# A hybrid encoder: the band's mask written into the bias rows, and the product of output and gate queued behind the product of weights and 1/z

## The chip, the cores and the metric

The kernel runs as one program on one core of one Trainium2 chip. The metric is the device time of one execution in microseconds (us), median of three runs. TensorE (PE, with its weight loads, PEld), VectorE (DVE), ScalarE (ACT), GpSimd (POOL) and SyncE (SP) each work through a queue of their own in order; semaphores tie them together. Almost all DMAs are issued by SP.

## The reference

The reference computes a two-layer encoder over x (1024 tokens x 1024 features), with 256 memory tokens. Layer 0 projects the normalised input to three groups of heads and a gate. Group A is banded attention: token i sees token j only where |i-j| <= 128, each head has a learned sink logit, and a relative-position bias (a table of 32 buckets x 6 heads) is added. Group B is dense attention with rotary positions, group X attention into the memory. What the change touches is this:

```python
rel = c - BLOCK - a                       # key minus query, c in 0..383, a in 0..127
bias = rel_bias_lookup(table, rel)
valid = ((jnp.abs(rel) <= WINDOW)[None] & (kpos >= 0)[:, None, :] & (kpos < S)[:, None, :])
logits = jnp.where(valid[None, :, None, None], logits + bias, NEG_INF)
...
p = jax.nn.softmax(jnp.concatenate([logits, sink_col], axis=-1), axis=-1)[..., :-1]
y = jnp.concatenate([y_a, y_b, y_x], axis=-1) * jax.nn.silu(gate)
return x + y @ w_out
```

Layer 1 has a differential attention (group C), with the same bias over all keys, and again X. A last RMS norm ends it.

## The kernel before, in words

Every projection is a chain of 24 fp32r matmuls of 512 columns into `acc` (high part of the activations with high part of the weights, and two cross terms, line 329). The weights come by DMA as `wr`, and are split into `wh` (DVE, line 241) and `wl` (mostly POOL, line 243). The projections are cut into pieces that the loop `run_steps` lays between the steps of attention, so that PE has work while a step's softmax runs on DVE, ACT and POOL. Once they are done, pieces of layer 0's output projection (`pre`, line 702) take their place.

A step of group B (`b_step`) handles one head and one block of 128 queries: scores into `sb` on PE, the minimum `mn` on DVE, the exponential `e` with its sum `z` on ACT, `rz` = 1/z on DVE and then the product `e` = `e` x `rz` (128x1024) on POOL, line 1114. SP copies `e` to `er`, PE transposes it (`te`), ACT and DVE split the result into `PTh` and `PTl`, and every second step PE multiplies with V (`ob`). A step of group A (`a_step`) does this for two query blocks over at most 384 keys each: scores `sa`, on DVE in one instruction the bias `ab` and the minimum (line 1184), on ACT the exponential, on POOL two products with `rz` (line 1198). There are three buffers of `e`; one is free again when the DMA to `er` that reads it has landed.

`y_evac` empties the output accumulator: ACT copies one half, DVE adds the other into `yt`, and POOL multiplies `yt` with the gate `gy` in place (line 473). After the second head of a pair `store_y` writes the gate tile out as `ysc`; the output projection reads it back as `yr` and splits it into `yh` (ACT) and `yl` (DVE).

The bias: a one-hot matrix turns the negated table into one vector of 512 values per head (`vp`, `vs`, `vec_d`). `skew(h)` writes that vector 128 times into `skew_d[h]` in DRAM, and a read with a row pitch of 511 gives each query its shifted row. For group A `a_bias(h)` reads 384 columns into `ab` and adds a 128x384 mask (0 in the band, 1e30 outside) on POOL, line 1152, six times in all. Layer 1 reads the same rows, without a mask, into `toep`.

Inside a step the order is: `s1` (scores, minimum, exponential), pieces of projections, `s3` of an earlier step (which ends with `y_evac`), `s2` of another (transposes and splits), then `finish` (1/z and the product with it), and pieces again. The order on each engine comes from a scheduler that starts from this order; `tc.issue_after(x)` tells it to put an instruction behind x. Each DMA bears one of eight semaphore lanes in turn and SP issues a DMA only when the one eight before it is done.

Of the kernel before, what the change touches and what calls it, by code (L numbers as in the profile page):

```python
# [41 lines left out]
PRE = ((((2, 3, 4, 5), 4), ((6,), 6), ((7,), 6)), (((2, 3), 6), ((4,), 6)))  # L42
SPARE = 24
LATE = 22
# [111 lines left out]
def encoder_kernel(ctx, tc, A):  # L156
# [35 lines left out]
    nsink = const.tile([P, 6], F32, name="nsink")  # L192
    tab = const.tile([32, 6], F32, name="tab")
    edge = pool(ctx, "edge", "right").tile([P, 120], F32, name="edge")
    spare = const.tile([P, SPARE], F32, name="spare")
    for t in (spare, edge):
# [14 lines left out]
            for l in range(2)]  # L211
    vec_d = dr.tile([6, 512], F32, name="vec_d")
    skew_d = dr.tile([6, P, 512], F32, name="skew_d")

# [252 lines left out]
    def y_evac(M, acc, gt, hr, c0, n=256):  # L467
        a = slice(hr * 64, hr * 64 + 64)
        b = slice(64 - hr * 64, 128 - hr * 64)
        t = M.at.tile([P, 256], F32, tag="yt", name="yt", bufs=2)  # L470
        nc.scalar.copy(t[a, :n], acc[b, :n])
        nc.vector.tensor_tensor(out=t[a, :n], in0=acc[a, :n], in1=t[a, :n], op=ALU.add)
        nc.gpsimd.tensor_tensor(out=gt[a, c0:c0 + n], in0=t[a, :n], in1=gt[a, c0:c0 + n], op=ALU.mult)

    def run_steps(steps, jobs, hooks=None, pace=None):
# [4 lines left out]
        for i in range(n + LAG + 1):  # L480
# [37 lines left out]
            if finish:  # L518
                with (tc.issue_after(behind.ins) if behind is not None else nullcontext()):
                    finish()  # L520
                finish = None
            if jobs is not None:
                jobs.pull(f // 2)
                if hooks:
                    hooks(-1)
# [510 lines left out]

    dma(tab, A["rel_bias"])
    nc.vector.tensor_scalar(out=tab, in0=tab, scalar1=-1.0, scalar2=None, op0=ALU.mult)
    oh = sg(M, "oh", F32)[:32, :]
    dma(oh, A["onehot"])  # L1040
    vp = ps_t("vp")
    nc.tensor.matmul(vp[0:6, :], tab, oh, start=True, stop=True)
    vs = sg(M, "vs", F32)[:6, :]
    nc.vector.tensor_copy(vs, vp[0:6, :])
    dma(vec_d, vs)
# [34 lines left out]
    if True:  # L1080
        def b_step(h, qb):
# [8 lines left out]
            def s1(h=h, qb=qb, e=e):  # L1090
# [20 lines left out]
                def finish():  # L1111
                    rz = stat("rz")
                    nc.vector.reciprocal(rz, z)  # L1113
                    nc.gpsimd.tensor_tensor(out=et, in0=et, in1=rz.to_broadcast([P, 1024]), op=ALU.mult)  # L1114
                    e[0] = et
# [4 lines left out]
            if st.sub == 1:  # L1120
                def s3(h=h, qb=qb, grp=grp):
                    ph, pl_ = grp["pt"]
                    acc = ps_a("ob")[:, :256]
                    n = 0
                    for kt in range(8):
                        for pt in (ph, pl_):
                            nc.tensor.matmul(acc, B["v"][:, kt, h // 3, :], pt[:, kt, :],
                                             start=(n == 0), stop=(n == 15))
                            n += 1
                    y_evac(M, acc, gates[3 + h // 2], h % 2, (qb - 1) * P)  # L1130
                    if h % 2 == 1 and qb == 7:
                        store_y(0, KORD[0].index(3 + h // 2), gates[3 + h // 2])
                st.s3 = s3
                st.need3 = ("bv", "g%d" % (3 + h // 2))
# [5 lines left out]
    def open_ab():  # L1140
        top_stack.close()
        ab = pool(top_stack, "ab", "right")
        mask = ab.tile([P, 384], F32, name="mask")
        dma(mask, A["mask"])
        abias["mask"], abias["pool"] = mask, ab
        M.xpool, M.xbufs = ab, XB

    def a_bias(h):
        mask = abias["mask"]
        t = abias["pool"].tile([P, 384], F32, tag="ab", name="ab", bufs=2)  # L1150
        dma(t, skew_src(h))
        nc.gpsimd.tensor_tensor(out=t, in0=t, in1=mask, op=ALU.add)
        abias[h] = t

    if True:
        def a_step(h, p):
# [5 lines left out]
            def s1(h=h, p=p, e=e):  # L1162
# [27 lines left out]
                def finish():  # L1190
                    rz = stat("rz2", 2)
                    nc.vector.reciprocal(rz, z)
                    for j in range(2):
# [3 lines left out]
                        ej = et[:, j, c:c + hi - lo]  # L1197
                        nc.gpsimd.tensor_tensor(out=ej, in0=ej, in1=rz[:, j:j + 1].to_broadcast([P, hi - lo]), op=ALU.mult)
                    e[0] = et
# [25 lines left out]
            def s3(h=h, p=p, grp=grp):  # L1225
# [15 lines left out]
                if h % 2 == 1 and p == 3:  # L1241
                    store_y(0, KORD[0].index(h // 2), gates[h // 2])
            st.s3 = s3
# [9 lines left out]
    def hooks0(i):  # L1253
        if 2 <= i < 8:
            skew(i - 2)
        if i < 0:
            wout_hook(0, jobs, "g2", r1)
# [7 lines left out]
    def out_proj(l, hT_next, stack, ahead=None):  # L1265
# [50 lines left out]
        for i, t in enumerate(order):  # L1316
# [31 lines left out]
            if tail:  # L1348
                nc.scalar.activation(xs[:, 0:384], xs[:, 0:384], AF.Identity, scale=r)
                nc.vector.tensor_scalar(out=xs[:, 384:1024], in0=xs[:, 384:1024], scalar1=r, scalar2=None,  # L1350
                                        op0=ALU.mult)
                nc.scalar.dma_start(out=out_d[rows, 0:384], in_=xs[:, 0:384])
                dma(out_d[rows, 384:1024], xs[:, 384:1024])
            elif l == 0:
# [281 lines left out]
def _constants():  # L1636
# [16 lines left out]
    b = np.where(rel > 0, 16, 0) + np.where(n < 8, n, large)  # L1653
    onehot = (np.arange(32)[:, None] == b[None, :]).astype(np.float32)
    r = np.arange(384)[None, :] - 128 - np.arange(128)[:, None]
    mask = np.where(np.abs(r) <= 128, 0.0, 1e30).astype(np.float32)
    return dict(cosT=cosT, sinT=sinT, onehot=onehot, mask=mask)

# [15 lines left out]
```

## Time and profile before

| | |
|---|---|
| three runs | 1227.74 us median (1226.81 to 1227.98) |
| the profiled execution | 1230.69 us |
| its span, first to last instruction | 1228.9 us |
| outside the span in it | 1.8 us |
| PE / DVE / ACT / POOL busy | 1196.5 / 801.1 / 663.1 / 436.3 us |

The span is cut in engines' busy time and waits. A view of waits names who waited for whom; a timeline lists instructions by start, with the idle time in front of each and what ended it in square brackets; a table of windows gives each engine's busy time in a stretch, and the mean clock granted to PE (1.00 is 2.4 GHz; its lower level is 1.2 GHz).

### The profile page before, as it was taken

The numbers are of one execution on the slowest core, as the hardware profiler recorded it, in microseconds if no ns is written. First come the engines' busy times: TensorE is split into PE (matmuls) and PEld (weight loads), VectorE is DVE, ScalarE is ACT, GpSimd is POOL, SyncE is SP. The second block draws the span as 40 slices with busy tenths as digits, with TensorE's granted clock in tenths as the row PEclk, the third lists the DMA queues.
The fourth block names the chain that finished last, engine by engine and source line by source line (L and its number), as shares of the span: only waits on it lengthen the run. The fifth ranks groups of instructions, "written<-read, shape, count | busy, mean of one in ns | idle before, by whom it ended". The sixth has DMA issues, their size and how long they took to land.

```text
span 1228.9 us, 19560 instructions
## 1 busy us (share of the span) xinstructions
PE 1196.5 (97%) x6614; PEld 988.4 (80%) x6614; DVE 801.1 (65%) x1495; ACT 663.1 (54%) x1477; POOL 436.3 (36%) x414
## 2 busy tenths in 40 slices
PE   6999999999999999999999999999999999999997
PEld 5788888888888777888888777777787777777886
DVE  5547665377778878635365866766767767667544
ACT  6248754366667766636157744555545454445332
POOL 5023365366665455437112222333143231301100
PEclk9999999999999999999999999999999999999999
DMA  6664445545465565457645445355363452468354
GB/s 257 200 194 147 163 172 163 166 160 207 163 233 209 208 227 191 151 196 237 186 158 156 153 146 164 121 183 163 124 187 125 153 171 105 149 212 285 121 192 155
DMA packets 114304, 216.70 MB, mean 176 GB/s; under 512 B 13302, under 2 KB 47478, under 8 KB 114204
## 3 DMA queue, kind: packets, MB, share of 16 engines
q1 hardware_dynamic: 114060, 215.25, 52.5%
q8 instruction: 53, 0.87, 0.3%
q14 instruction: 47, 0.39, 0.1%
q10 hardware_dynamic: 144, 0.20, 0.0%
HBM read 87.71 MB, written 39.86 MB: 104 GB/s over the span
## 4 chain that ended last, share of the span: by engine, by line
PE 47%; DVE 2%; DMA 1%; issue 1%; ACT 1%; POOL 0%; POOLq 0%; SPq 0%; DVEq 0%; ACTq 0%
PE acc L329 24%; PE po L702 5%; PE oc L1545 3%; PE sc L1505 3%; PE te L580 3%; PE sc L1514 2%; PE pre L702 2%; PE oc L1547 2%; DMA wr<-in_w_in 1%; PE ssqc L1563 1%; PE ox L656 0%; PE rbcc L1576 0%; PE tv L439 0%; PE sx L543 0%; DVE e L1520 0%
## 5 line engine op out<-in xcount | busy, mean ns | idle before, releaser
L329 PE MATMUL acc<-h,wh 128*128 128x512 f32 x1536 | 499.5, 398 | 1.6 <-DVE h L351 0.8
L329 PEld LDWEIGHTS acc<-h,wh 128*128 128x128 f32 x1536 | 282.4, 188 | 65.7 <-issue 7.9
L329 PE MATMUL acc<-h,wl 128*128 128x512 f32 x768 | 303.8, 396 | 1.5 <-POOL wl L243 1.2
L243 POOL TENSOR_TENSOR wl<-wr,wh 128x512 fp32r<-128x512 f32 x94 | 124.8, 1329 | 286.3 <-DVE wh L241 155.0
L1523 ACT ACTIVATE e<-e,mn 128x1024 f32<-128x1024 f32 x96 | 110.0, 1148 | 117.0 <-DVE mn L1520 116.9
L329 PEld LDWEIGHTS acc<-h,wl 128*128 128x128 f32 x768 | 144.3, 188 | 34.9 <-issue 4.4
L1114 POOL TENSOR_TENSOR e<-e,rz 128x1024 f32<-128x1024 f32 x48 | 91.6, 1910 | 84.2 <-DVE rz L1113 57.8
L1520 DVE CUSTOM_DVE_ANT_0 e<-sc,toep 128x1024 f32<-128x1024 f32 x96 | 113.5, 1218 | 8.0 <-PE sc L1514 7.3
L580 PEld LDWEIGHTS te<-identr,er 128*128 128x128 f32 x896 | 92.2, 143 | 18.8 <-PE sa L543 2.2
L580 PE MATMUL te<-identr,er 128*128 128x128 f32 x896 | 99.9, 246 | 4.3 <-DVE O L1578 1.4
L348 DVE TENSOR_TENSOR PT<-te,PT 128x512 fp32r<-128x512 f32 x112 | 74.3, 687 | 42.8 <-ACT PT L347 39.2
L241 DVE CAST wh<-wr 128x512 fp32r<-128x512 f32 x112 | 58.2, 522 | 42.9 <-PE acc L329 17.3
L348 DVE TENSOR_TENSOR PTl<-te,PTh 128x512 fp32r<-128x512 f32 x112 | 74.0, 684 | 9.4 <-ACT PTh L347 8.9
L1545 PE MATMUL oc<-PT,v 128*128 128x512 f32 x192 | 69.8, 403 | 0.7 <-DVE ckl L1420 0.7
L1532 DVE SCALAR_TENSOR_TENSOR e<-e,mr 128x1024 f32<-128x1024 f32 x48 | 66.3, 1381 | 1.5
L347 ACT CAST PT<-te 128x512 fp32r<-128x512 f32 x112 | 62.7, 589 | 7.2 <-PE te L580 6.7
L347 ACT CAST PTh<-te 128x512 fp32r<-128x512 f32 x112 | 62.2, 586 | 7.9 <-PE te L580 7.1
L702 PE MATMUL po<-woh,yh 128*128 128x512 f32 (+1 forms) x172 | 65.7, 382 | 0.0
L702 PE MATMUL po<-woh,yl 128*128 128x512 f32 (+1 forms) x172 | 65.5, 381 | 0.0
L702 PE MATMUL po<-wol,yh 128*128 128x512 f32 (+1 forms) x172 | 65.3, 380 | 0.0
L1105 DVE TENSOR_REDUCE mn<-sb 128x1 f32<-128x1024 f32 x48 | 58.3, 1216 | 7.0 <-PE sb L543 6.6
L350 ACT ACTIVATE yh<-yr 128x256 fp32r<-128x256 f32 (+2 forms) x56 | 24.0, 447 | 66.2 <-DMA yr<-ysc 37.5
(211 smaller groups left out, 2358.7 us busy)
## 6 DMA issues: line engine op xcount, KB each, us to landing
er<-e SPq DMA_DIRECT2D x112, 512.0 KB, 3.0
wr<-in_w_in SPq DMA_DIRECT2D x96, 256.0 KB, 3.0
ysc<-gy SPq DMA_DIRECT2D x16, 512.0 KB, 2.7
cq<-sg SPq DMA_DIRECT2D x64, 128.0 KB, 2.5
ck<-sg SPq DMA_DIRECT2D x48, 128.0 KB, 2.3
er<-e SPq DMA_DIRECT2D x12, 384.5 KB, 2.6
xpsc<-xh SPq DMA_DIRECT2D x18, 256.0 KB, 2.6
xr<-xpsc SPq DMA_DIRECT2D x9, 512.0 KB, 3.6
```

The costliest lines, as they stand in the source:

```text
L243: (nc.vector if fast else nc.gpsimd).tensor_tensor(out=lo, in0=raw, in1=hi, op=ALU.subtract)
L329: lastmm[0] = nc.tensor.matmul(acc, a, b[:, k, c0:c0 + n], start=(i == 0), stop=(i == 23))
L347: nc.scalar.copy(hi, src)
L348: return nc.vector.tensor_tensor(out=lo, in0=src, in1=hi, op=ALU.subtract)
L580: nc.tensor.transpose(to[:, i * P:(i + 1) * P], e[0][:, k * P:(k + 1) * P], idt)
L702: lastmm[0] = nc.tensor.matmul(acc, a, b, start=(start and n == 0), stop=(stop and n == 2))
L1105: nc.vector.tensor_reduce(out=mn, in_=Sp, op=ALU.min, axis=AX.X)
L1114: nc.gpsimd.tensor_tensor(out=et, in0=et, in1=rz.to_broadcast([P, 1024]), op=ALU.mult)
L1520: nc.vector.tensor_tensor_reduce(out=et, in0=Sp, in1=toeps[h][:, w0:w0 + 1024], scale=1.0, scalar=BIG, op0=ALU.add, op1=ALU.min, accum_out ...
L1523: nc.scalar.activation(et, et, AF.Exp, bias=mn[:, m:m + 1], scale=-1.0, accum_out=z[:, m:m + 1])
L1532: nc.vector.scalar_tensor_tensor(out=es[0], in0=es[1], scalar=c, in1=es[0], op0=ALU.mult, op1=ALU.add)
L1545: nc.tensor.matmul(acc, V[:, kt, 0, :], ph.both[:, kt, :], start=(kt == 0), stop=(kt == 7), skip_group_check=True)
```

## The change

There are four edits. The mask moves into the bias vector: the table becomes 33 rows x 12 columns (the six heads twice; row 33 is 0 for the first six and, once negated, 1 for the last six), the one-hot matrix gets a row 33 with 0 in the band and 1e30 outside, and so the matmul makes six plain and six masked vectors. `skew` writes twelve tiles; A reads the masked ones, and the add and the mask tile are gone. The product of output and gate, and the store behind it, are held in a list `late` and are issued after the step's `finish`, behind the last product with `rz`. `spare` gets smaller by what `tab` grows, so that all other tiles keep their addresses. And the last store of the result goes out on SP in both its parts, 640 columns first; before, ACT issued the part of 384 columns.

```diff
-SPARE = 24
+SPARE = 16
-    tab = const.tile([32, 6], F32, name="tab")
+    tab = const.tile([33, 12], F32, name="tab")
-    vec_d = dr.tile([6, 512], F32, name="vec_d")
-    skew_d = dr.tile([6, P, 512], F32, name="skew_d")
+    vec_d = dr.tile([12, 512], F32, name="vec_d")
+    skew_d = dr.tile([12, P, 512], F32, name="skew_d")
...
-        nc.gpsimd.tensor_tensor(out=gt[a, c0:c0 + n], in0=t[a, :n], in1=gt[a, c0:c0 + n], op=ALU.mult)
+        def mult():
+            with (tc.issue_after(lastw[0].ins) if lastw[0] is not None else nullcontext()):
+                nc.gpsimd.tensor_tensor(out=gt[a, c0:c0 + n], in0=t[a, :n], in1=gt[a, c0:c0 + n], op=ALU.mult)
+        late.append(mult)
+    late, lastw = [], [None]
...
+            while late:
+                late.pop(0)()
...
-    dma(tab, A["rel_bias"])
+    for i in range(2):
+        dma(tab[:32, 6 * i:6 * i + 6], A["rel_bias"])
+    dma(tab[32:33, :], A["onehot"][32:33, 512:524])
-    nc.tensor.matmul(vp[0:6, :], tab, oh, start=True, stop=True)
+    nc.tensor.matmul(vp[0:12, :], tab, oh, start=True, stop=True)
...
-                    nc.gpsimd.tensor_tensor(out=et, in0=et, in1=rz.to_broadcast([P, 1024]), op=ALU.mult)
+                    lastw[0] = nc.gpsimd.tensor_tensor(out=et, in0=et, in1=rz.to_broadcast([P, 1024]), op=ALU.mult)
-                        store_y(0, KORD[0].index(3 + h // 2), gates[3 + h // 2])
+                        late.append(lambda: store_y(0, KORD[0].index(3 + h // 2), gates[3 + h // 2]))
...
-        mask = ab.tile([P, 384], F32, name="mask")
-        dma(mask, A["mask"])
-        dma(t, skew_src(h))
-        nc.gpsimd.tensor_tensor(out=t, in0=t, in1=mask, op=ALU.add)
+        dma(t, skew_src(6 + h))
...
-            skew(i - 2)
+            skew(6 + i - 2)
+        if 10 <= i < 16:
+            skew(i - 10)
...
-                nc.scalar.dma_start(out=out_d[rows, 0:384], in_=xs[:, 0:384])
-                dma(out_d[rows, 384:1024], xs[:, 384:1024])
+                for h in (slice(384, 1024), slice(0, 384)):
+                    dma(out_d[rows, h], xs[:, h])
```

The order on PE and on DVE stays as it was, but for the sizes of the bias vectors' instructions. On POOL the six adds go, and only from the last of them on does the order of the rest change. There, near the end of layer 0's attention, the rows before were these (`e<-e,rz` is the product with 1/z, `gy<-yt,gy` that with the gate):

```order
L1198 TENSOR_TENSOR e<-e,rz_5053 128x256
L473 TENSOR_TENSOR gy<-yt,gy 64x256
L1152 TENSOR_TENSOR ab<-ab,mask 128x384
L473 TENSOR_TENSOR gy<-yt,gy 64x256
L1114 TENSOR_TENSOR e<-e,rz 128x1024 x2
L1198 TENSOR_TENSOR e<-e,rz_5237 128x256
L1198 TENSOR_TENSOR e<-e,rz_5237 128x384
```

and now they are:

```order
L1205 TENSOR_TENSOR e<-e,rz_5053 128x256
L476 TENSOR_TENSOR gy<-yt,gy 64x256
L1125 TENSOR_TENSOR e<-e,rz 128x1024
L476 TENSOR_TENSOR gy<-yt,gy 64x256
L1125 TENSOR_TENSOR e<-e,rz 128x1024
L1205 TENSOR_TENSOR e<-e,rz_5237 128x256
L1205 TENSOR_TENSOR e<-e,rz_5237 128x384
```

The add is gone, and the second product with the gate stands behind the first of the two products with 1/z. From there on each product with the gate stands behind the product with 1/z that it stood in front of, where it did.

On SP, in the first steps of attention (group X, which has no products with 1/z on POOL), the writes of `skew_d` and the loads of weights stood so:

```order
L175 DMA skew_d<-vec_d 128x512 x5
L175 DMA wr<-in_w_in 128x512 x2
L175 DMA er<-e 128x1024
L175 DMA wr<-in_w_in 128x512 x2
L175 DMA er<-e 128x1024
```

and now stand so:

```order
L175 DMA skew_d<-vec_d 128x512 x5
L175 DMA wr<-in_w_in 128x512 x2
L175 DMA skew_d<-vec_d 128x512 x2
L175 DMA er<-e 128x1024
L175 DMA skew_d<-vec_d 128x512
L175 DMA wr<-in_w_in 128x512
L175 DMA skew_d<-vec_d 128x512 x2
L175 DMA wr<-in_w_in 128x512
L175 DMA skew_d<-vec_d 128x512
L175 DMA er<-e 128x1024
```

Five of the six new writes stand in front of the second half of the next weight tile.

Also on SP, near the end of layer 0's attention, the store of a pair of heads and the loads of it stood so:

```order
L175 DMA ysc_94<-gy 128x1024
L175 DMA xpsc_97<-xh 128x512
L175 DMA er<-e 128x769
L175 DMA er<-e 128x1024
L175 DMA xh<-in_x 128x512
L175 DMA yr<-ysc_94 128x2x128
L175 DMA er<-e 128x1024
L175 DMA xpsc_97<-xh 128x512
L175 DMA yr<-ysc_94 128x4x128
```

and now:

```order
L175 DMA xpsc_97<-xh 128x512
L175 DMA ysc_94<-gy 128x1024
L175 DMA er<-e 128x769
L175 DMA er<-e 128x1024 x2
L175 DMA xh<-in_x 128x512
L175 DMA xpsc_97<-xh 128x512
L175 DMA yr<-ysc_94 128x2x128
L175 DMA yr<-ysc_94 128x4x128
```

The first load of `yr` now waits behind a store of `xpsc` (a finished piece of the output projection) that it stood in front of.

## Rows read from the trace of the kernel before

**Rows 1.** The page's busy time by engine, share of the span.
```profile
PE 1196.5 (97%) x6614; PEld 988.4 (80%) x6614; DVE 801.1 (65%) x1495; ACT 663.1 (54%) x1477; POOL 436.3 (36%) x414
```

**Rows 2.** PE's waits, 100 to 600 us: us in total, times, longest.
```profile
PE sa L543 <- DVE mn L1184: 3.7, 3, 2.2
```

**Rows 3.** Windows: busy PE, PEld, DVE, ACT, POOL (instructions), PE clock, DMA share, GB/s.
```profile
75.00:80.00 5.00, 5.00 (x27) 4.29 (x26) 1.99 (x3) 3.15 (x10) 0.00 (x0) 1.00 0.98 329
...
300.00:350.00 50.00, 50.00 (x312) 43.51 (x311) 38.29 (x76) 34.53 (x83) 31.04 (x28) 1.00 0.49 176
...
435.00:440.00 5.00, 3.16 (x23) 2.65 (x21) 1.19 (x5) 2.12 (x6) 4.76 (x4) 1.00 0.50 201
440.00:445.00 5.00, 4.61 (x22) 4.18 (x23) 3.71 (x10) 2.47 (x7) 0.83 (x2) 0.66 0.68 240
```

**Rows 4.** Timeline of PE around two waits: start, us, instruction, [idle before, releaser].
```profile
437.77 0.39 PE L543 MATMUL sb<-bkl,q 128*128 128x512 f32 x1
440.39 0.69 PE L543 MATMUL sa<-ak,q 128*128 128x384 f32 x1 [2.23 <-DVE mn L1184]
...
464.77 0.39 PE L543 MATMUL sa<-ak,q 128*128 128x256 f32 x1 [1.07 <-DVE mn L1184]
```

**Rows 5.** Timeline of DVE, the same stretch.
```profile
432.15 0.15 DVE L1113 RECIPROCAL rz<-z 128x1 f32<-128x1 f32 x1
432.23 0.67 DVE L290 TENSOR_TENSOR wol<-wor,woh 128x512 fp32r<-128x512 f32 x1
...
439.70 0.62 DVE L1184 CUSTOM_DVE_ANT_0 e<-sa,ab,nsink 128x384 f32<-128x384 f32 x1 [3.04 <-DMA er<-e]
```

**Rows 6.** Timeline of SP, the same stretch.
```profile
436.59 2.32 SPq L175 DMA_DIRECT2D er<-e  x2
```

**Rows 7.** Timeline of POOL, the same stretch.
```profile
432.21 1.56 POOL L1152 TENSOR_TENSOR ab<-ab,mask 128x384 f32<-128x384 f32 x1 [3.79 <-DMA ab<-skew_d]
433.85 0.73 POOL L473 TENSOR_TENSOR gy<-yt,gy 64x256 f32<-64x256 f32 x1
434.67 3.75 POOL L1114 TENSOR_TENSOR e<-e,rz 128x1024 f32<-128x1024 f32 x2
```

**Rows 8.** The six adds of the mask: ns min/median/max, first and last start.
```profile
L1152 POOL TENSOR_TENSOR ab<-ab,mask x6: 1008/1017/1564, 218.7 to 432.2; 128x384 f32<-128x384 f32 x6
```

**Rows 9.** Timeline of POOL, two products beside a split on DVE.
```profile
405.99 1.89 POOL L1114 TENSOR_TENSOR e<-e,rz 128x1024 f32<-128x1024 f32 x1 [2.95 <-issue]
...
421.27 2.21 POOL L1114 TENSOR_TENSOR e<-e,rz 128x1024 f32<-128x1024 f32 x1 [3.64 <-issue]
```

**Rows 10.** Timeline of DVE, the split beside the first of these.
```profile
406.08 2.35 DVE L290 TENSOR_TENSOR wol<-wor,woh 128x512 fp32r<-128x512 f32 x1 [0.22 <-ACT woh L289]
```

**Rows 11.** Timeline of SP where the new writes go in.
```profile
70.55 3.06 SPq L175 DMA_DIRECT2D skew_d<-vec_d  x5
...
81.80 2.04 SPq L175 DMA_DIRECT2D wr<-in_w_in  x2
```

**Rows 12.** The writes of skew_d: us from issue to landing.
```profile
DMA to landing us min/median/max: 4.2/4.5/6.2
```

**Rows 13.** Timeline of DVE, the cast of the second half of those weights.
```profile
86.54 0.43 DVE L241 CAST wh<-wr 128x512 fp32r<-128x512 f32 x1 [1.68 <-DMA wr<-in_w_in]
```

**Rows 14.** Timeline of PE, the next wait behind that cast.
```profile
95.12 1.05 PE L833 MATMUL ssq<-small,sq 128*128 128x2 f32 x8 [0.22 <-DVE PTl L348]
```

**Rows 15.** Timeline of SP, the first load of yr and the store of xpsc behind it.
```profile
451.46 0.72 SPq L175 DMA_DIRECT2D yr<-ysc  x1
...
454.33 0.32 SPq L175 DMA_DIRECT2D xpsc<-xh  x1
```

**Rows 16.** Timeline of ACT, the split that reads it.
```profile
461.14 0.42 ACT L350 ACTIVATE yh<-yr 128x256 fp32r<-128x256 f32 x1
```

**Rows 17.** Timeline of the last stores of the result.
```profile
1217.07 8.15 SPq L175 DMA_DIRECT2D out<-xs  x2
...
1224.95 0.38 ACTq L1352 DMA_DIRECT2D out<-xs  x1
```

More of the change, by code (lines that the diff above doesn't have):

```diff
@@ L1033, in encoder_kernel @@
             dma(memT_d[i][:, 4 * j:4 * j + 4, :], memT[i].tiles[j])
-    dma(tab, A["rel_bias"])
+    for i in range(2):
+        dma(tab[:32, 6 * i:6 * i + 6], A["rel_bias"])
+    dma(tab[32:33, :], A["onehot"][32:33, 512:524])
     nc.vector.tensor_scalar(out=tab, in0=tab, scalar1=-1.0, scalar2=None, op0=ALU.mult)
-    oh = sg(M, "oh", F32)[:32, :]
-    dma(oh, A["onehot"])
+    oh = sg(M, "oh", F32)[:33, :]
+    dma(oh, A["onehot"][:, 0:512])
     vp = ps_t("vp")
-    nc.tensor.matmul(vp[0:6, :], tab, oh, start=True, stop=True)
-    vs = sg(M, "vs", F32)[:6, :]
-    nc.vector.tensor_copy(vs, vp[0:6, :])
+    nc.tensor.matmul(vp[0:12, :], tab, oh, start=True, stop=True)
+    vs = sg(M, "vs", F32)[:12, :]
+    nc.vector.tensor_copy(vs, vp[0:12, :])
     dma(vec_d, vs)
@@ L1142, in open_ab @@
         ab = pool(top_stack, "ab", "right")
-        mask = ab.tile([P, 384], F32, name="mask")
-        dma(mask, A["mask"])
-        abias["mask"], abias["pool"] = mask, ab
+        abias["pool"] = ab
         M.xpool, M.xbufs = ab, XB
     def a_bias(h):
-        mask = abias["mask"]
         t = abias["pool"].tile([P, 384], F32, tag="ab", name="ab", bufs=2)
-        dma(t, skew_src(h))
-        nc.gpsimd.tensor_tensor(out=t, in0=t, in1=mask, op=ALU.add)
+        dma(t, skew_src(6 + h))
         abias[h] = t
@@ L1197, in finish @@
                         ej = et[:, j, c:c + hi - lo]
-                        nc.gpsimd.tensor_tensor(out=ej, in0=ej, in1=rz[:, j:j + 1].to_broadcast([P, hi - lo]), op=ALU.mult)
+                        lastw[0] = nc.gpsimd.tensor_tensor(out=ej, in0=ej, in1=rz[:, j:j + 1].to_broadcast([P, hi - lo]), op=ALU.mult)
                     e[0] = et
@@ L1241, in s3 @@
                 if h % 2 == 1 and p == 3:
-                    store_y(0, KORD[0].index(h // 2), gates[h // 2])
+                    late.append(lambda: store_y(0, KORD[0].index(h // 2), gates[h // 2]))
             st.s3 = s3
@@ L1653, in _constants @@
     b = np.where(rel > 0, 16, 0) + np.where(n < 8, n, large)
[L1654 to L1657, printed above, removed]
+    onehot = np.zeros((33, 524), np.float32)
+    onehot[:32, :512] = np.arange(32)[:, None] == b[None, :]
+    onehot[32, :512] = np.where(n <= 128, 0.0, 1e30)
+    onehot[32, 518:] = -1
+    return dict(cosT=cosT, sinT=sinT, onehot=onehot)
 def kernel(**inputs):
```

## The prediction

> **What bounds the kernel now.** I read the page's busy time first: PE is busy for 97% of the span, no other engine for more than 65% [rows 1]. Time can be won only where PE waits or runs at its lower clock, so the view of PE's waits comes next. Between 100 and 600 us, where everything in this change but its first and last DMAs lies, one line leads: the scores of group A (`sa`) waited three times for DVE's line 1184, 3.7 us in all, the longest 2.2 us [rows 2]. The windows then show where PE has no slack to give: from 300 to 350 us it is busy for 50.00 of 50 us [rows 3], although the six adds of the mask are spread over 218.7 to 432.2 us, about 1.0 us each [rows 8]. In most of its six places the add is thus paid by nobody.
>
> The last of the six is another matter. In 435 to 440 us PE is busy for only 3.16 us, and in the next window its clock is 0.66 on average [rows 3]. The timelines give the chain, and the reader should follow it backwards. PE's `sa` starts at 440.39 after 2.23 us of idleness; its work before it ended at 437.77 + 0.39 = 438.16 [rows 4]. It waited for DVE's line 1184, which started at 439.70 and itself stood 3.04 us waiting for a DMA `er<-e`, because only then was a buffer of `e` free to write into [rows 5]. SP issued that copy at 436.59 [rows 6], which is 3.11 us before 439.70. The copy had to wait for POOL's product of `e` with 1/z: the first of the two that start at 434.67 takes half of 3.75 us and ends at 436.55 [rows 7]. And this product was late not for its operand, since `rz` started at 432.15 and took 0.15 us [rows 5]; POOL was standing in the add of the mask, which began at 432.21 after 3.79 us of waiting for its own DMA and took 1.56 us, and then in the product with the gate, 0.73 us [rows 7].
>
> **The change, part by part.**
>
> *The add and the gate's product at 432 us.* Both leave the front of that first product. It then starts when `rz` is there: 432.30, and 0.13 us for the signal. Its duration is 1.89 to 2.21 us [rows 9]; I take 2.21, since DVE has just begun a split of two operands at 432.23 [rows 5], the situation of the 2.21. So it ends at 434.64 instead of 436.55, and the copy is issued 1.9 us sooner. With the same 3.11 us to DVE, `sa` starts at 438.5, against PE's own readiness at 438.16: the wait shrinks from 2.23 to about 0.35 us, a gain of 1.9. What is late next is the same chain; its floor for PE is the 438.16.
>
> *The clock behind it.* A mean of 0.66 over 440 to 445 [rows 3] between levels of 1.0 and 0.5 means 3.4 us at the half, so 1.7 us of work lost. At the wait of 1.07 us at 464.77 [rows 4] I see no such drop, so a wait of 0.35 us should keep the full clock. The bounds are 0 (the clock falls all the same) and 1.7; the nearer row is the shorter wait, so 1.7. The two gains together: 3.6 us.
>
> *The other five adds.* Their POOL time goes, some 5 us, but PE waits for none of it [rows 3]. I take 0. DVE's line 1184 now waits for the DMA of `ab` itself, which landed well before each use, as the add did.
>
> *The order of the gate's products elsewhere.* Up to 425 us POOL's order is the same without the adds. Later, each product with the gate passes behind one with 1/z; those that gave way are 0.73 us long [rows 7], and PE waited for none of the others there except at 464.77, where the wait comes from DVE. 0, with 0.7 us of gain as the other end.
>
> *Six more writes of `skew_d`.* Five of them stand before the second half of the weight pair that SP issues from 81.80 to 83.84 [rows 11]. SP's issue of five such writes took 3.06 us [rows 11] and fits into its idle time. But the 16 DMA engines were full from 75 to 80 us, 0.98 busy at 329 GB/s [rows 3], at which rate a write of 256 KB takes 0.8 us. DVE already stands 1.68 us for that half at 86.54 [rows 13], and the score minimum behind that cast feeds exponentials, casts and splits without a gap, up to PE's `ssq` at 95.12, which waits 0.22 us for them [rows 14]. So what the weights lose, PE loses. The lower end is 0: the DMA engines drain between 80 and 84 us. The upper end: all five writes at up to 1.7 us each (five of them landed within 6.2 us of the last issue [rows 12], 8.6 us after the first), which is rival 3. Two writes are issued directly before the half, 1.6 us of transfer at the full rate, and start some 1.2 us earlier; I take 0.5 us of loss.
>
> *The table and vectors.* Two more small loads and twelve rows in place of six; the matmul still has 512 columns. 0: the loads were issued 10 us before they are used.
>
> *The last store.* SP's second store of the last rows was issued in a group that ends at 1217.07 + 8.15 = 1225.22 [rows 17]; ACT issued its part at 1224.95 beside it. Now the smaller part comes behind, 1225.22 instead of 1224.95, with nothing left to hide it: a loss of 0.3 us, between 0 (the larger part lands last anyway) and 0.6 us (its 192 KB alone at 329 GB/s).
> The Trainium skill (DMA: Bandwidth & Descriptors, Issuing engines are not separate DMA queues) says that DMAs from either engine run on the same 16 DMA engines, and that a second issuer saves only issue time. By that rule the price is the 0.3 us of issue; if ACT's queue had moved its data on its own, it would be the 0.6. No row here separates the two.
>
> **Sum.** -1.9 - 1.7 + 0.5 + 0.3 = -2.8 us. On the profiled execution's own time, span 1228.9 and 1.8 around it, that is 1230.7 - 2.8 = 1227.9. That execution was 3.0 us longer than the median of the runs, 1227.74, with which the change will be compared: 1227.74 - 2.8 = 1224.9 us.
>
> **Rivals.**
>
> *1. More is won.* The other waits of `sa` on line 1184 (3.7 - 2.23 = 1.5 us [rows 2]) shrink as well, because POOL is less often in the way. For it: the same line, the same kind of buffer. Against it: at 464.77 I find DVE, not POOL, late. 1224.9 - 1.5 = 1223.4 us.
>
> *2. POOL's product, now earlier, stalls DVE.* The product of 405.99 us kept a split on DVE that began 0.09 us later busy for 2.35 us instead of 0.67 [rows 5, 9, 10]. If the freed product gets in front of the split of 432.23, DVE is 1.7 us later with line 1184 for the step before, and PE waits some 1.5 us for that at about 434.5. For it: the two now start within 0.2 us of each other. Against it: `rz` signals after the split has started, and then POOL is the one that stretches. 1224.9 + 1.5 = 1226.4 us.
> The Trainium skill (GPSIMD Engine Reference, 1. Specifications) says POOL's SBUF interfaces are shared with VectorE and contend with DVE instructions that have two SBUF inputs. By that rule one of the two must stretch; the trace agrees, with 2.35 us beside 0.67.
>
> *3. Slower: the writes of `skew_d` hold up the weights.* If a write costs the DMA engines 1.7 us and not 0.8, five cost 8.5 us; the backlog from 80 us then reaches past 88, and the second half of the weights lands 3.6 us later. PE waits 3.8 us at 95.12 and the clock falls, 1.7 us more as above. In place of my 0.5 us stand 5.3 to 5.9 us: 1224.9 - 0.5 + 5.5 = 1229.9 us. It decides from about 1.2 us per write, where the queue no longer drains before 81.8. For it: the 0.98 of the engines, and writes that land after 4.2 to 6.2 us [rows 12]. Against it: 329 GB/s were moved just while five of them ran.
>
> *4. It doesn't do what it says.* The wait at 440.39 stays, because another buffer or the moved store sets it. The first `yr` load passes behind a store of `xpsc`, from 451.46 to 454.7 [rows 15]; its reader on ACT comes at 461.14 [rows 16], 6.4 us later, so I don't see it there. The time would be 1227.74 + 0.8 = 1228.5 us.
>
> **Chances and range.** A measurement of this kernel can tell about 0.2%, 2.5 us, from no change, so faster means below 1225.3 and slower above 1230.2. Forecast 0.52, with a range of its own of 1223.9 to 1225.9, about two thirds of it below 1225.3; rival 1 0.14; rival 2 0.16; rival 3 0.14, somewhat over half of it above 1230.2; rival 4 0.04. Faster: 0.36 + 0.14 = 0.50. Slower: 0.08. The same: 0.42. The range goes from 1222.8, a little under rival 1, to 1228.2, which leaves out most of rival 3.
>
> **What would show it.** Right: around 432 to 440 us (shifted by up to 0.5) POOL goes from `rz` straight into the product, the copy `er<-e` is issued about 2 us after it, PE's wait at that `sa` is below 0.6 us and the clock of the following window is 1.00; at the first `ssq` of line 833 PE waits under 1 us; the last store starts about 0.3 us after the one before it. Wrong: the wait at that `sa` is still over 1 us, or a new wait of over 1 us stands between 434 and 520 us, or the wait at 95 us is above 1.5 us with the clock below 1.00 behind it, or the gain in 400 to 520 us is there and the rest of the program has lost it.

## The result, and the profile after

The changed kernel takes 1231.36 us in the median of 10 runs (1229.16 to 1234.84), the kernel before 1227.24 us (10 runs, 1224.51 to 1228.99). The ratio is 1.0039, with a 95% interval of 1.0027 to 1.0050: slower by some 4 us. Forecast were 1224.9 us and a range of 1222.8 to 1228.2; the result lies outside it, on the side of rival 3 (1229.9).

PE's waits in the changed kernel, first from 60 to 130 us, then from 100 to 600 (line waited for: us in total, times, longest):

```profile
PE ssq L841 <- DVE PTl L348: 3.7, 1, 3.7
...
PE sa L551 <- DVE mn L1191: 2.2, 4, 1.1
```

The first line was 0.22 us [rows 14], the second 3.7 us with a longest of 2.2 [rows 2]. So both changes of which the prediction spoke are there: the loss at 95 us and a shorter wait at 440 us. The windows of the two kernels show where the first comes from (columns as in [rows 3]; the last three are PE's clock, the busy share of the DMA engines and GB/s). Before:

```profile
80.00:85.00 5.00, 5.00 (x37) 4.53 (x35) 2.45 (x5) 3.51 (x11) 2.58 (x3) 1.00 0.32 104
85.00:90.00 5.00, 5.00 (x28) 4.30 (x27) 1.98 (x3) 1.80 (x8) 2.57 (x2) 1.00 0.63 209
```

and after:

```profile
75.00:80.00 5.00, 5.00 (x28) 4.28 (x27) 1.91 (x2) 3.21 (x11) 0.00 (x0) 1.00 0.95 279
80.00:85.00 5.00, 5.00 (x36) 4.56 (x35) 2.57 (x4) 3.31 (x11) 2.60 (x2) 1.00 0.90 307
85.00:90.00 5.00, 5.00 (x28) 4.25 (x27) 0.61 (x2) 0.25 (x1) 1.29 (x1) 1.00 0.94 249
...
95.00:100.00 5.00, 1.72 (x9) 1.72 (x9) 2.59 (x4) 4.13 (x8) 0.00 (x0) 0.85 0.00 0
100.00:105.00 5.00, 5.00 (x12) 3.94 (x13) 2.23 (x4) 2.48 (x9) 3.31 (x2) 0.50 0.31 120
```

The engines' pause at 80 to 85 us (0.32) is filled (0.90), and the next five microseconds too. SP's timeline of the changed kernel (start, us of issue) shows the new writes around the loads of the two halves of the weight pair (`wr`):

```profile
75.75 1.11 SPq L175 DMA_DIRECT2D skew_d<-vec_d  x2
76.96 0.54 SPq L175 DMA_DIRECT2D er<-e  x1
77.55 0.60 SPq L175 DMA_DIRECT2D skew_d<-vec_d  x1
82.03 0.33 SPq L175 DMA_DIRECT2D wr<-in_w_in  x1
82.41 1.11 SPq L175 DMA_DIRECT2D skew_d<-vec_d  x2
83.75 0.40 SPq L175 DMA_DIRECT2D wr<-in_w_in  x1
```

DVE's timeline shows the casts that wait for the two halves, and PE's what follows:

```profile
85.72 0.43 DVE L241 CAST wh<-wr 128x512 fp32r<-128x512 f32 x1 [2.83 <-DMA wr<-in_w_in]
89.81 0.43 DVE L241 CAST wh<-wr 128x512 fp32r<-128x512 f32 x1 [3.67 <-DMA wr<-in_w_in]
```

```profile
94.18 0.40 PE L329 MATMUL acc<-h,wh 128*128 128x512 f32 x1
98.28 1.72 PE L841 MATMUL ssq<-small,sq 128*128 128x2 f32 x8 [3.71 <-DVE PTl L348]
99.86 0.77 PE L329 MATMUL acc<-h,wh 128*128 128x512 f32 x1
```

The second cast starts at 89.81 in place of 86.54 [rows 13], 3.27 us later; PE waits 3.71 us and then runs at half its clock (a product of 128x512 takes 0.63 to 0.77 us in place of 0.40) until 105.4. What PE lost is read from its lag: the start of one PE instruction in this trace, less the start of the same instruction in the first trace of before. The lag is -0.32 us at 72 us and +5.90 at 115.

At 440 us POOL, SP and PE of the changed kernel did what the prediction said:

```profile
436.37 2.21 POOL L1125 TENSOR_TENSOR e<-e,rz 128x1024 f32<-128x1024 f32 x1 [4.02 <-ACT mr L1120]
438.66 0.74 POOL L476 TENSOR_TENSOR gy<-yt,gy 64x256 f32<-64x256 f32 x1
```

```profile
438.61 3.26 SPq L175 DMA_DIRECT2D er<-e  x2
```

```profile
442.65 0.44 PE L551 MATMUL sa<-ak,q 128*128 128x384 f32 x1 [0.57 <-DVE mn L1191]
```

`rz` started at 436.08; the copy goes out 2.53 us behind it in place of 4.44 [rows 5, 6], and PE waits 0.57 us in place of 2.23 [rows 4]; the clock stays at 1.00. PE's lag falls by 4.2 us from 395 to 510 us. The two traced executions differ by 1.05 us (1231.74 and 1230.69), the medians by 4.1. Why a gain that the trace shows is missing in the medians is the second question.

### The profile page after: what moved, and what is told of

It is laid out like the page before. It is cut to its first block, busy times and chain, and to the rows that moved or that the text cites. A ratio compares the mean times of both kernels' runs of the same rounds, so it can differ in the third digit from the quotient of the medians.

```text
span 1229.7 us, 19563 instructions
## 1 busy us (share of the span) xinstructions
PE 1196.2 (97%) x6614; PEld 987.8 (80%) x6614; DVE 801.0 (65%) x1495; ACT 663.1 (54%) x1477; POOL 430.3 (35%) x408
## 4 chain that ended last, share of the span: by engine, by line
PE 57%; DVE 2%; issue 2%; DMA 1%; ACT 1%; POOL 1%; SPq 0%; POOLq 0%; DVEq 0%; ACTq 0%
PE acc L329 23%; PE po L710 9%; PE pre L710 4%; PE sc L1514 3%; PE oc L1554 3%; PE te L588 3%; PE sc L1523 2%; PE oc L1556 2%; PE ob L1138 1%; DMA wr<-in_w_mem 1%; PE ox L664 1%; PE tx L377 1%; DMA wr<-in_w_in 1%; PE sb L551 1%; PE ssqc L1572 1%
```

## Experiments

On the loss, theory A: the added writes make it. Theory B: it lies elsewhere (late product, late stores, tail). On the gain, theory C: the stall at 440 us in the kernel before stands in some executions only. D: it stands in all. Theories A1 and A2 are about the parts of the gain: the removed add, or the late product. A run is compared with the kernel before timed beside it; the kernel before has medians of 1225.65 to 1227.40 us in these series.

**The writes moved.** The changed kernel, with the six plain writes behind copies of `e` at steps 30 to 35 (the lines that keep each copy's instruction in `laster` are left out here).

```diff
-        if 10 <= i < 16:
-            skew(i - 10)
+        if 30 <= i < 36:
+            with tc.issue_after(laster[0].ins):
+                skew(i - 30)
```

> The changed kernel, with the six plain writes of skew_d queued behind copies of e at steps 30 to 35 (about 300 us) in place of 75 to 85 us; everything else as changed. Theory A (the writes hold up the weights, PE waits 3.7 us at ssq and then runs at half clock; PE's work stands 5.9 us later behind it): the wait at the first ssq is below 0.5 us, the clock stays at 1.00 from 95 to 110 us, and the time is 1231.4 - 5.9 = 1225.5 us. Theory B (the loss sits elsewhere, in the late product with the gate, the late stores or the tail, and a wait removed at 95 us comes back later): the time stays within 1.5 us of 1231.4.

Measured: 1225.46 us (12 runs), beside 1226.29 for the kernel before; the ratio is 0.9998 (0.9988 to 1.0008) in place of 1.0039. Each beside its own series of before, this kernel is 0.8 us faster and the changed one 4.1 slower, so the move is worth some 5 us. The clock is 1.00 behind `ssq`, and PE's wait there:

```profile
95.20 1.05 PE L841 MATMUL ssq<-small,sq 128*128 128x2 f32 x8 [0.23 <-DVE PTl L348]
```

The loss is the writes', and A stands; but no gain is left over that can be told from none.

**The writes alone, in the kernel before**, into a tensor that nobody reads.

```diff
+    skew_e = dr.tile([6, P, 512], F32, name="skew_e")
...
+        if 10 <= i < 16:
+            dma(skew_e[i - 10], bass.AP(vec_d.tensor, vec_d.offset + (i - 10) * 512, [[0, P], [1, 512]]))
```

> The kernel before, with six more writes of 256 KB out of vec_d into a tensor that nobody reads, at the changed kernel's place in the program (75 to 85 us); mask adds, products and stores as before. Theory A: a wait of 3 to 4.5 us at the first ssq, the clock at 0.5 behind it, the time 1227.2 + 5.9 = 1233 us. Theory B: no more than 1 us over 1227.2.

Measured: 1231.87 us beside 1226.29, ratio 1.0059 (1.0045 to 1.0073), and at `ssq`:

```profile
97.48 1.18 PE L834 MATMUL ssq<-small,sq 128*128 128x2 f32 x8 [2.84 <-DVE PTl L349]
```

A again, in a kernel that has nothing else of the change. Then three of them (`i < 13`), and six of a quarter of the width (`[1, 128]`):

> The kernel before with three more writes of 256 KB at the changed kernel's place (75 to 85 us) in place of six; two of them and the third stand before the second half of the weight pair. If each write costs the same (six gave a wait of 2.8 to 3.7 us at ssq and 5.6 us in the median), three give a wait of 1.4 to 2 us with a shorter clock drop and about 1229.5 us. If the DMA engines drain before the weights as forecast, and only a larger number overruns them, three give a wait below 0.6 us and 1226.5 to 1227 us.

> The kernel before with six more writes at the changed kernel's place, each of 128 rows of 512 bytes in place of 2 KB: a quarter of the bytes, as many rows and as many issues. If bytes on the 16 DMA engines make the delay (rival 3 of the prediction), the wait at ssq is below 1 us and the time within 1.5 us of 1226.5. If the issues on SP or the number of rows make it, the wait is 2.8 to 3.7 us and the time 1231 to 1232 us, as with the wide writes.

Measured: three, 1229.42 us beside 1227.40 (1.0013, 1.0001 to 1.0024), wait 1.14 us, PE 2.1 us later at 115; narrow, 1227.96 us beside 1227.40 (1.0008, 0.9997 to 1.0020), wait 0.65 us. As many rows and issues with a quarter of the bytes cost 0.6 us in place of 5.6, and 0.6 can't be told from none: it is the bytes and not the number of rows or issues. The wait with three writes has its like in a repeat of the kernel before (1.02 us, below), and so has PE's loss; that three cost something shows in the median alone, and barely.

**The parts of the gain.** The kernel with the writes moved, with the product and the stores of a head's output back in their old place, so that the mask in the bias rows is alone (the two lines of the stores are left out here):

```diff
-        late.append(mult)
+        mult()
...
```

> As the first of these (mask in the bias rows, plain writes at 300 us), but the product with the gate and the stores of a head's output stand again where they stood before, ahead of the product with 1/z. Theory A1 (the removed add alone gives the gain at 432 to 440 us, since it was 1.56 us and waited 3.79 us for its DMA): within 0.8 us of the first of these, PE's wait for sa at about 440 us below 1 us. Theory A2 (the order of the two products gives it): 1.5 us or more slower than the first, with a wait for sa above 1.5 us between 430 and 445 us.

Measured: 1225.07 us beside 1226.29, 0.9996 (0.9986 to 1.0005); wait for `sa` 0.7 us. A1: the removed add is what shortens that wait. The late product alone, in the kernel before, with the add of the mask kept (the lines for `late`, `lastw` and the stores are as in the change):

```diff
-        nc.gpsimd.tensor_tensor(out=gt[a, c0:c0 + n], in0=t[a, :n], in1=gt[a, c0:c0 + n], op=ALU.mult)
+        def mult():
+            with (tc.issue_after(lastw[0].ins) if lastw[0] is not None else nullcontext()):
+                nc.gpsimd.tensor_tensor(out=gt[a, c0:c0 + n], in0=t[a, :n], in1=gt[a, c0:c0 + n], op=ALU.mult)
+        late.append(mult)
...
```

> The kernel before with the late product and the late stores alone: mask adds, six writes and the last store as before. The late product by itself takes 0.73 us from in front of the product with 1/z at 432 us, but the add of the mask stays in front. Theory A1 (the add makes the stall): PE's wait for sa at 440 us is 1.2 to 2.2 us and the time within 1 us of 1226.3, the median of the kernel before. Theory A2 (the order of the products makes it): wait below 0.6 us, 2 to 3 us faster.

Measured: 1227.05 beside 1226.72 us, 0.9996 (0.9988 to 1.0005); wait 1.3 us, full clock behind it. POOL's timeline shows the add of 1.56 us still in front and the product next:

```profile
431.32 1.56 POOL L1160 TENSOR_TENSOR ab<-ab,mask 128x384 f32<-128x384 f32 x1 [3.79 <-DMA ab<-skew_d]
432.85 1.89 POOL L1122 TENSOR_TENSOR e<-e,rz 128x1024 f32<-128x1024 f32 x1
```

A1, for the most part: the late product takes 0.9 us off the wait of 2.2 that the first trace shows, the mask alone 1.5.

**The last store** back on two queues, in the kernel with the writes moved:

```diff
-                for h in (slice(384, 1024), slice(0, 384)):
-                    dma(out_d[rows, h], xs[:, h])
+                nc.scalar.dma_start(out=out_d[rows, 0:384], in_=xs[:, 0:384])
+                dma(out_d[rows, 384:1024], xs[:, 384:1024])
```

> The kernel with the mask in the bias rows, the late product and the plain writes at 300 us, and with the last store given back to ACT's queue as in the kernel before (both parts issued side by side). If the single issuer cost 0.3 us as forecast (bounds 0 and 0.6), the median is about 1225.2 us beside 1225.5 of the same kernel with both stores on SP, and in the trace the end of the span stands 0.3 us sooner behind the last normalisation. If the larger part lands last anyway, the two are equal. A difference of 0.3 us is below what the medians tell; the trace's tail decides.

Measured: 1226.86 us beside 1226.72, 0.9998 (0.9990 to 1.0007). From the start of DVE's last scaling to the end of the span pass 4.3 us, as in the changed kernel; over all traces it is 4.3 to 4.6 with one issuer (three traces) and 4.2 to 4.6 with two (thirteen). The single issuer costs nothing that shows in this spread.

**The kernel before again**, unedited, for its trace:

> The kernel before once more, for a second trace of it. The first trace ran 1230.7 us where the median of the runs is 1227.2. Theory C (the wait of 2.23 us for sa at 440 us, with the clock drop behind it, stands in some executions only): no wait over 1 us there and a time near 1227. Theory D (it is there each time, so that the change wins it each time): a wait of 1.8 to 2.6 us for sa at 440 us and a clock of about 0.66 in the 5 us behind it.

> The kernel before, a third trace. Both traces so far (1230.7 and 1228.9 us) have the wait of 2.2 us for sa at 440 us and the clock of 0.66 behind it, and both are longer than the median of 1226.3 us. Theory C (the stall belongs to the longer executions): a trace near 1226 us has a wait below 1.5 us and no drop of the clock there. Theory D (it is always there): wait 2.2 us and clock 0.66, whatever the time.

> The kernel before, a fourth trace, for the same question: theory C, a trace near 1226 us without the wait of 2.2 us at 440 us; theory D, the wait of 2.2 us and the clock of 0.66 whatever the time.

> The kernel before once more, timed in rounds against itself. Its four traces ran 1228.0 to 1230.7 us where the medians are 1226.3 and 1226.7. If the traced execution of this kernel is a slower one than those timed in rounds, this run's traced execution is again above 1228 us while its median is within 0.5 us of the other's, and the gain read from the trace at 440 us is too large for the timed runs. If the four were chance, the traced execution lies anywhere in 1224.5 to 1229.

Measured: 1228.93, 1228.01 and 1229.43 us (one run each), and in rounds 1226.83 beside 1227.40 us (0.9995, 0.9985 to 1.0005; its traced execution 1226.85, no slower than the timed ones). C: two of these four traces, the second and fourth of before, have PE's wait of 2.2 us and the clock at 0.66 and 0.68, as the first; the third and the one in rounds have 1.2 us and 1.00. The stall does not go by the length of the execution: the third, at 1228.01 us, is without it. What sets the two forms apart is seen on POOL and DVE. The second trace (wait 2.23 us):

```profile
431.30 1.55 POOL L1152 TENSOR_TENSOR ab<-ab,mask 128x384 f32<-128x384 f32 x1 [3.80 <-DVE PTl L348]
```

```profile
431.22 0.15 DVE L1113 RECIPROCAL rz<-z 128x1 f32<-128x1 f32 x1
431.29 0.67 DVE L290 TENSOR_TENSOR wol<-wor,woh 128x512 fp32r<-128x512 f32 x1
```

and the one timed in rounds (wait 1.23 us):

```profile
431.77 1.01 POOL L1152 TENSOR_TENSOR ab<-ab,mask 128x384 f32<-128x384 f32 x1 [3.68 <-DMA ab<-skew_d]
```

```profile
431.82 0.15 DVE L1113 RECIPROCAL rz<-z 128x1 f32<-128x1 f32 x1
431.89 1.43 DVE L290 TENSOR_TENSOR wol<-wor,woh 128x512 fp32r<-128x512 f32 x1
```

Where DVE's reciprocal starts first, by 0.06 to 0.17 us, and its split follows without a gap, the add takes 1.45 to 1.56 us and DVE's split 0.67; where the add starts before the reciprocal, by 0.05 to 0.11, it takes 1.01 and the split 1.4. So it is in all eight traces of the kernel before and of it with added writes, four of each kind. To settle whether the order decides, the sixth add was pushed behind the reciprocal:

```diff
+        if h == 5:
+            w = abias["pool"].tile([P, 64], F32, name="abw")
+            nc.gpsimd.tensor_copy(w, t[:, 0:64])
         nc.gpsimd.tensor_tensor(out=t, in0=t, in1=mask, op=ALU.add)
```

> The kernel before with a small copy of 128x64 on POOL, reading the same bias rows, directly ahead of the sixth add of the mask, so that this add always starts after DVE's reciprocal at 432 us. If the engine that starts first decides which of the two is stretched, the add takes 1.4 to 1.6 us and DVE's split 0.67 us, PE waits 2.2 to 2.6 us for sa and the clock falls behind it in this trace, as in the four traces where DVE was first, and the median is 1.5 to 3 us above that of before, since all executions then have the long wait. If something else decides, the wait is 1.2 us or 2.2 us as it falls, plus 0.2 to 0.4 us for the copy, and the median within 1 us of before.

POOL's timeline of this run, and its window behind the wait:

```profile
430.53 0.24 POOL L1154 COPY abw<-ab 128x64 f32<-128x64 f32 x1 [3.60 <-DMA ab<-skew_d]
430.85 1.44 POOL L1155 TENSOR_TENSOR ab<-ab,mask 128x384 f32<-128x384 f32 x1
```

```profile
440.00:445.00 5.00, 5.00 (x34) 4.16 (x33) 4.43 (x10) 4.32 (x10) 1.57 (x3) 1.00 0.62 220
```

The reciprocal started at 430.67: the add is second and takes 1.44 us, and PE waits 2.22 us, as in the traces where it came second by itself. The order sets the wait, as expected. But the clock stayed at 1.00, against the expectation: after waits of 2.1 to 2.2 us it falls in four traces of five. The median is 1227.26 beside 1225.65 us (1.0010, 0.9998 to 1.0021), without one execution of 4007.55 us, which nothing here explains: in the direction forecast, not beyond doubt.

**The add gone without a write added.** A third buffer, each bias a head sooner:

```diff
-        t = abias["pool"].tile([P, 384], F32, tag="ab", name="ab", bufs=2)
+        t = abias["pool"].tile([P, 384], F32, tag="ab", name="ab", bufs=3)
...
-                if p == 1 and h < 5:
+                if p == 0 and h < 5:
                     a_bias(h + 1)
```

(the call stands behind the step's scores)

> The kernel before with a third buffer for the bias rows, so that each head's load and its add of the mask come a head earlier and no add stands at 432 us; no write of skew_d is added and the product with the gate keeps its place. If the add there makes the wait of 1.2 or 2.2 us for sa, the wait is below 0.8 us, the clock keeps 1.00 in 440 to 445, and PE gains over 395 to 510 us what the kernels with the mask in the rows gain there (2.8 to 4.5 us against the first trace of before). In the median that is worth 1 to 2 us if half of the timed executions have the longer wait (about 1225.5 us beside 1226.5 to 1227.4), under 1 us if most have the shorter one. If the add is not the cause, wait and time stay as before.

Measured: 1225.05 beside 1225.65 us, 0.9993 (0.9983 to 1.0003), wait 0.68 us. The add is the cause of the wait here too. The gain is 0.6 us in the median, below what can be told from none.

**All twelve writes late**, the rest as with the mask alone, and the last store on two queues:

```diff
-        if 2 <= i < 8:
-            skew(6 + i - 2)
+        if 10 <= i < 16:
+            with tc.issue_after(laster[0].ins):
+                skew(6 + i - 10)
...
```

> The mask in the bias rows with the products in their old order and the last store on two queues as before, and all twelve writes of skew_d away from the weights: the masked ones behind the copies of e at steps 10 to 15, the plain ones at steps 30 to 35. If the five writes that the kernel before already issues at 70 to 73 us also hold up the weights (its waits at ssq were 0.2, 0.6, 1.0 and 0.2 us in four traces, up to 2 us lost behind them), the wait is 0.2 us or gone and the median is 0.5 to 2 us below 1226.5; if not, the time is that of the kernel with the plain writes late alone, 1225 to 1226 us.

Measured: 1226.44 beside 1227.40 us, 0.9985 (0.9974 to 0.9996), the one version that its interval puts below the kernel before. The unedited copy had 0.9995 in the same comparison, so some 0.4 us (1226.83 - 1226.44) are left: no version here beats the kernel before by 0.2%. The wait at `ssq` is 0.2 us, but so it is in three of the five traces of before, and the question of this run, whether the first five writes cost something too, stays open.

## Why the prediction was wrong

The table gives the change of PE's lag against the first trace of before (as defined above; us) over three stretches of that trace, and PE's longest wait for `sa` between 425 and 446 us. The sixth add stands at 432 us.

| trace | 72 to 115 | 395 to 432 | 432 to 510 | wait, clock behind it |
|---|---|---|---|---|
| before, second | 0.4 | -1.5 | 0.0 | 2.2, low |
| before, third | 1.9 | -1.4 | -1.5 | 1.2, full |
| before, fourth | 0.0 | -1.5 | 0.0 | 2.2, low |
| before, in rounds | 0.0 | -1.3 | -1.5 | 1.2, full |
| add pushed back | 0.0 | -1.6 | -1.2 | 2.2, full |
| six writes more | 3.8 | -1.2 | -1.5 | 1.2, full |
| three writes more | 2.1 | 0.1 | -0.1 | 2.1, low |
| six narrow writes more | 0.4 | -1.4 | -1.5 | 1.2, full |
| late product alone | 0.0 | -0.8 | -1.6 | 1.3, full |
| bias sooner | 0.0 | -0.7 | -2.4 | 0.7, full |
| changed | 6.2 | -1.9 | -2.3 | 0.6, full |
| writes moved | 0.0 | -1.9 | -2.5 | 0.4, full |
| mask alone | 2.2 | -1.1 | -2.8 | 0.7, full |
| two stores | 0.0 | -0.5 | -2.3 | 0.6, full |
| all twelve late | 0.0 | -0.8 | -2.7 | 0.8, full |

*Six more writes of `skew_d`: taken 0.5, the upper end 5.3 to 5.9, measured 6.2 in the trace. This step failed.* The sum priced the two writes directly in front of the second half of the weights at 1.6 us and took off a head start of 1.2. The casts of the two halves show what they cost. In the kernel before the first half was cast at

```profile
84.44 0.43 DVE L241 CAST wh<-wr 128x512 fp32r<-128x512 f32 x1 [1.52 <-DMA wr<-in_w_in]
```

and the second at 86.54 [rows 13]; in the changed kernel it was 85.72 and 89.81. With six writes more in the kernel before:

```profile
84.47 0.43 DVE L242 CAST wh<-wr 128x512 fp32r<-128x512 f32 x1 [1.80 <-DMA wr<-in_w_in]
89.01 0.43 DVE L242 CAST wh<-wr 128x512 fp32r<-128x512 f32 x1 [4.12 <-DMA wr<-in_w_in]
```

and with three, none of which stands between the halves:

```profile
85.67 0.43 DVE L242 CAST wh<-wr 128x512 fp32r<-128x512 f32 x1 [2.72 <-DMA wr<-in_w_in]
87.62 0.43 DVE L242 CAST wh<-wr 128x512 fp32r<-128x512 f32 x1 [1.53 <-DMA wr<-in_w_in]
```

Without a write between the halves the casts start 1.9 to 2.2 us apart in twelve traces, 2.8 in the thirteenth (all twelve late). With two writes between them it is 4.1 and 4.5 us, with one narrow write 2.5. So the two writes cost 2.0 to 2.4 us, 1.0 to 1.2 each, and of the head start nothing is left: when they were issued, from 82.41 on, the first half, issued at 82.03, was itself still on its way (its cast waits until 85.72). The other three writes, in front of the first half, can have made at most the 1.3 us by which that half is later in the changed kernel; with six writes more it is not later at all (84.47), and with three alone both halves come as in the third trace of before (85.47 and 87.47), which has none of them. What they cost is not shown. Nor are all 6.2 us the writes': without an added write this stretch varies from 0.0 to 2.2 us by itself (before, third; mask alone).

The price of a write on the engines, 0.8 us, was near. The DMA view from 66 to 100 us (queue: packets, MB, share of the 16 engines), before and after:

```profile
q1 hardware_dynamic: 3073, 5.88, 51.7%
```

```profile
q1 hardware_dynamic: 3690, 6.75, 66.2%
```

That is 14.5% of 34 us, 4.9 us more, for six writes more and one load of the same size fewer in that stretch: an estimate of 0.8 to 1.0 us each.

From the 3.27 us on, it went as in rival 3: PE's wait grew by 3.5 us and the clock fell, which the forecast had left out at this place. It cost the rest of the 6.2, 2.7 us, in place of rival 3's 1.7. The prediction's own sign of being wrong (a wait above 1.5 us at 95 us with the clock below 1.00 behind it) is what the trace shows. Rival 3's reason, five writes at over 1.2 us each, did not hold: the two between the halves made most of it.

*Add and product: taken -1.9. The clock behind it: taken -1.7.* The chain is right: the wait fell by 1.66 us, with the product at 2.21 us as taken, and the clock stays up. But 2.3 us are won from 432 us on, not 3.6, and the other kernels without the add win 2.3 to 2.8. Both terms are too large even on the first trace. The drop of the clock costs 1.2 us: with the wait at 2.2 us in both, PE is at 0.0 with the drop and at -1.2 without it (add pushed back). And a wait of 1.2 us in place of 2.2 is worth only 0.3 (-1.5 beside -1.2): where the add is first, DVE's split takes 0.7 us longer, and PE loses 0.6 to 0.7 us to that at 434 to 437 us, before it comes to the wait.

The rest of the 4.2 us that the changed kernel's trace gains from 395 to 510 lies in front of 432 us, and most of it is not the change's. The first trace of before has a second drop of the clock there, behind a wait of 1.41 us for `PTh` that the repeats have as well (1.31 to 1.43 us):

```profile
420.00:425.00 5.00, 5.00 (x25) 4.52 (x26) 3.22 (x9) 3.17 (x10) 2.21 (x1) 0.67 0.35 104
```

In the same window the four repeats have a clock of 1.00, and so they gain 1.3 to 1.5 us on the first trace in front of the add.

*The median.* The sum was made on an execution 3.0 us above the median and then taken off the median. Part of these 3.0 us were the two drops: the trace of before that ran at its median (1226.85 us) has neither, and is 2.8 us shorter in 395 to 510. (It also lacks 1.8 us at 930 to 950 us, where the first trace and that of the changed kernel wait 1.4 and 1.5 us for DVE's last product on `O`.) What the median does not have cannot be won from it. The clock at 440 us falls in four of the ten traces with the add at that place; where it does not fall, those with the add have -1.2 to -1.6 us from 432 on and those without it -2.3 to -2.8, so about 1.0 us is left to win. The medians can hardly tell that much, and agree with it in the main: with the plain writes late they are 0.8 and 1.2 us below before, and 0.1 us above it in the third comparison.

*The last store: taken +0.3.* Nothing that shows (4.3 us behind the last scaling, 4.6 in the first trace of before). By the Trainium skill (DMA: Bandwidth & Descriptors, Issuing engines are not separate DMA queues) a second issuer saves only the time of issue, here an estimated 0.3 us [rows 17]; the spread of 4.2 to 4.6 us hides that much, so the runs do not separate its rule from the other.

*The other adds, the order elsewhere: taken 0.* Right: the lag moves by 0.05 us from 115 to 395, and the wait at 464.77 is 1.06 us in place of 1.07.

Rival 1 did not happen (that 1.06 us stayed), nor rival 2 (the split beside the product, at 436.16, took 0.67 us, and the product 2.21), nor rival 4 (the wait at 440 us did shrink).

## What to carry to other kernels

A transfer that is needed much later still costs at the place where it is issued, if one that is needed soon is issued behind it: here two writes of 256 KB between the halves of a weight tile held up the second half by 1.0 to 1.2 us each, although they were issued up to 1.3 us ahead of it. So price what stands directly in front at its full time, without a head start, where another transfer is still under way as here. A stall read from one trace has its price in the median only if the median's execution has it: where two engines start within 0.1 us of each other, expect two forms, and look for a second trace before a clock drop is booked. And a shorter wait is not yet time won: here 1.0 us less of waiting was worth 0.3, because PE had lost the rest shortly before.

## What the runs showed of the hardware

- POOL's add of 128x384 and DVE's split of 128x512, which reads two operands, stretch each other, and the order decides which one pays. Where DVE's reciprocal, directly ahead of the split, starts before the add (by 0.05 to 0.18 us, six traces), the split keeps its 0.67 us and the add takes 1.44 to 1.56. Where the add starts before the reciprocal (by 0.05 to 0.11 us, four traces), the add keeps its 1.01 and the split takes 1.4. The Trainium skill (GPSIMD Engine Reference, 1. Specifications) has the two contend; these ten traces agree.
- The clock fell (0.78 to 0.80 in 95 to 100 us) behind waits at `ssq` of 1.0, 1.1 and 1.3 us in three traces (and behind 2.8 and 3.7), not behind 0.6 and 0.7 (the window of the third trace of before, behind 1.0, is below). At 440 us it fell behind 2.1 to 2.2 us in four of five, never behind 1.2 or 1.3. At 420 us it fell behind 1.41 us in the first trace of before and not behind 1.43 in the second. The length of a wait alone does not tell.

```profile
95.00:100.00 5.00, 4.05 (x18) 3.39 (x19) 3.73 (x7) 2.50 (x7) 2.62 (x2) 0.80 0.27 107
```

- The time around the span is nearly constant for each build: 1.79 us before, 1.88 with the mask alone, 2.05 in the changed kernel, 2.25 with the late product alone (means of 10 to 12 executions, standard deviations 0.03 to 0.05). It is 0.26 us of the loss; what sets it stays open.
